# Hybrid diffusion trunk on one core: the context queries of the even layer's attention issued inside the last HGRN unit, the output weights split during the latent queries

## The chip, the cores and the metric

The kernel runs on one NeuronCore of a Trainium2 chip. A core has five engines that each work through a queue of their own in order: TensorE (PE, matrix products into PSUM), VectorE (DVE), ScalarE (ACT), GpSimd (POOL) and SyncE (SP, which here only issues DMA transfers). They meet through semaphores. The metric is the device time of one execution in microseconds; lower is better. All matrix work is done in float32 by splitting an operand into a high part `hi` (rounded by a cast on ACT) and a low part `lo` (the difference, by a subtraction on DVE or POOL), and adding three products.

## The reference, cut to what matters

Two layers over 1024 latent tokens and 256 context tokens of width 1024. The change lies in the mixer of layer 0 (the even layer), where two mixers work side by side and one output projection joins them:

```
def attend(q, k, v):                          # mixer A: 8 query heads, 2 key heads, head size 64
    s = einsum("bqhgd,bkhd->bhgqk", q, k) * ATTN_SCALE
    p = softmax(s)
    return einsum("bhgqk,bkhd->bqhgd", p, v)
o_lat = attend(q_lat, concat(k_ctx, k_lat), concat(v_ctx, v_lat))   # latent queries: all 1280 keys
o_ctx = attend(q_ctx, k_ctx, v_ctx)                                 # context queries: 256 keys

def step(S, inp):                             # mixer B (HGRN2): 4 heads, both directions
    scores = einsum("bhtd,bhtsd,bhsd->bhts", qc, decay, kc)
    o = einsum("bhts,bhsv->bhtv", scores, vc) + einsum("bhtd,bhdv->bhtv", qc * exp(b), S)
    S_new = exp(b_last) * S + einsum("bhsd,bhsv->bhdv", kc * exp(b_last - b), vc)

y = concat([o_attention, rms_norm(o_hgrn) * silu(g)]) @ w_out       # for latent and context tokens
```

Then come a gated FFN, the odd layer and its FFN; none of them is touched.

## The kernel before

**Stages.** `even_in` holds the first 630 us: the token-major projections (`even_token_major`, which writes queries, keys and values to the DRAM scratch `q2d`, `k2d`, `v2d`) and the HGRN mixer (`hgrn`). `even_out` holds the attention and the output projection (`even_attention`), to about 1085 us. `second` is everything after.

**HGRN.** There are 12 units: 4 heads times three token blocks (context 256, latent 512, latent 512). For each unit, `project(u)` makes the products with the operands `xh`, `xl` (5 KB of each partition per 1280 tokens and eight slices, 80 KB in all) and the split weights; `chain(u)` runs the log-step scan within chunks of 128 tokens: seven levels (m = 1, 2, 4, ... 64), each with one product group on PE (tiles `h_pd`, `h_pa`), one copy `hKM` on ACT for m up to 16, and three products on DVE (`hK` L795, `hQ` L797, `hT` L798); then transposes `h_kt`, the masked sum `hA` (L824 to L836). `tail(u)` makes the chunk states (`h_ds`, `hds`, `hS` L928), the outputs `h_po`, the RMS norm over `h_ms`, `h_dg`, `h_bc` and the gating on POOL (L977), and stores to `hgd`. `chain(u)`, `tail(u - 1)` and `project(u + 1)` are issued in turns: a `yield` of one is followed by steps of the others. The last unit has no `project` beside it, so its chain and its tail are alone on the engines.

**Attention.** `even_attention` works through 40 pairs of (block of 256 queries, head): 8 context pairs first, then 32 latent ones. The loop runs over half-steps `s`; half-step `s` issues the scores of tile `s` (two tiles of 128 queries make a pair), the exponential of tile `s-1` (L1054, ACT), the transposes of pair `s//2 - 2` (`a_pt`), their split into `a_ph` (ACT) and `a_pl` (DVE L1082), the products with the values of pair `s//2 - 3` (`a_pv`), the division of tile `s-1` by its sum (reciprocal `rl` L1059 on DVE, scaling L1060 on POOL) and, at the end of a pair, `finish` (`pv_t` on ACT, `a_oT` on DVE L1111). The row maximum is taken by one DVE instruction that also moves the scores to SBUF (`a_p<-g_ps` or `a_p<-a_s`, L1047). Half-steps 0 to 15 are the context pairs (256 keys); half-step 16 is the first with latent queries (1280 keys). Two steps of the output projection (three products each) go into each half-step once a block's eight heads and its four HGRN slices (`a_g`, loaded from `hgd`) are split.

**Output weights.** `even_w_out` is split in 8 pieces: `load_w(m)` loads a 512 KB `w_raw`, `prepare_w(m)` casts `w_hi` on ACT (L1018) and subtracts `w_lo` on POOL (L1019), then issues `load_w(m + 2)`. Piece m is prepared in half-step 2m + 2, all within the context pairs. `w_raw` and `a_g` share a tag with two buffers.

**Order.** Inside `in_order(...)` every instruction of the engines named keeps the order in which the code issues it; between two such blocks a scheduler may move an instruction. `chained()` keeps the order of SP's transfers. A tile that takes over the memory of an earlier one waits until the last reader of that one is done. When `even_in` closes, `even_out` opens its pools over the same SBUF and PSUM.

Of the kernel before, what the change touches and what calls it, by code (L numbers as in the profile page):

```python
# [20 lines left out]
P = 128  # L21
# [44 lines left out]
class Trunk:  # L66
# [597 lines left out]
    def hgrn(self, xh, xl, gp):  # L664
# [73 lines left out]
        first, tp, pp, sp, mods = yield load, prepare, project  # L738
# [8 lines left out]
        def chain(u):  # L747
# [11 lines left out]
            pd = [pp.tile([P, 2, 5, 32], F32, name=f"h_pd{i}", bufs=1) for i in range((nch + 1) // 2)]  # L759
# [126 lines left out]
        with self.in_order(*self.compute):  # L886
# [6 lines left out]
            for u in range(len(units)):  # L893
                fill = project(u + 1) if u + 1 < len(units) else iter(())
# [13 lines left out]
                for _ in fill:  # L908
                    x += 1
                    if x % 2 == 0:  # L910
                        side()
            while tails:
                side()
            for _ in mods:
                pass
# [66 lines left out]
    def even_attention(self, gp, tp, pp, sp):  # L982
# [32 lines left out]
        def prepare_w(m):  # L1015
# [3 lines left out]
            nc.gpsimd.tensor_tensor(out=lo, in0=raw, in1=hi.bitcast(F32), op=OP.subtract)  # L1019
# [5 lines left out]
        def load_keys(g):  # L1025
            for s in range(2):
                k = K2[g, s] = sp.tile([P, NTOK], F32R, name=f"K2_{g}{s}", bufs=1)
                nc.sync.dma_start(k.bitcast(F32), self.k2d[g, s].bitcast(F32))
# [39 lines left out]
        def transposes(pair, half):  # L1068
# [66 lines left out]
        def project():  # L1135

            for b, (n0, kind) in enumerate(blocks):
                for i in range(2):
                    y = sp.tile([P, D], F32, name="y", bufs=2)
                    ms = self.small.tile([P, 2], F32, name="y_ms")  # L1140
                    for half in range(2):
# [11 lines left out]
                        if half == 0:  # L1153
                            xt = sp.tile([P, D], F32, name="y_x", bufs=2)
# [33 lines left out]
        nc.gpsimd.memset(zeros, 0.0)  # L1188
        N = 2 * len(pairs)
        E = mybir.EngineType  # L1190
        with self.in_order(*self.compute, E.SP):
            load_keys(0)
            load_q(0)
            load_q(1)
            load_keys(1)
            V = sp.tile([P, NT, AKV * P], F32R, name="V2", bufs=1)
            nc.sync.dma_start(V.bitcast(F32), self.v2d.rearrange("t p c -> p t c").bitcast(F32))
            load_w(0)
            load_w(1)
            load_gate(1)  # L1200
            for s in range(N + 8):
                pair, half = s // 2, s % 2
                if s < N:
                    if half == 0:
                        load_q(pair + 2)
                    scores(s)
                if 0 <= s - 1 < N:
                    exponential(s - 1)
                if 2 <= s < 18 and half == 0:
                    prepare_w(s // 2 - 1)  # L1210
                if 0 <= pair - 3 < len(pairs):
                    values(pair - 3, half)
                t = transposes(pair - 2, half) if 0 <= pair - 2 < len(pairs) else iter(())
                next(t, None)
                step(1)
                next(t, None)
                step(1)
                next(t, None)
                if 0 <= s - 1 < N:
                    divide(s - 1)  # L1220
                if 0 <= pair - 3 < len(pairs) and half == 1:
                    finish(pair - 3)
                for _ in range(min(len(todo), 1 + len(todo) // 3)):
                    todo.pop(0)()
# [1354 lines left out]
    def run(self, stages=5):  # L2579
        for f in (self.even_in, self.even_out, self.second)[:stages]:  # L2580
            f()
# [9 lines left out]
    def even_in(self):  # L2591
        nc, a, pool = self.nc, self.a, self.pool
        with ExitStack() as es:
            self.mc = pool(es, "modc")
            hp = pool(es, "h0")
            xh = hp.tile([P, KT, NTOK], F32R, name="xh")
            xl = hp.tile([P, KT, NTOK], F32R, name="xl")
            self.wp = pool(es, "weights", side="right")
            gp = pool(es, "g_psum", 2, space=PSUM)
# [159 lines left out]
```

## Time and profile before

| | |
|---|---|
| runs shown | 3350.71, 3346.67, 3350.41 us; median 3350.41 |
| the profiled execution | 3351.56 us; span of its trace 3349.8 us |
| TensorE | busy 3107.8 us (93% of the span), mean granted clock 0.967 |
| VectorE, ScalarE, GpSimd | busy 60%, 45%, 46% of the span |
| the chain that ended last | PE 73%, DVE 9%, ACT 4%, issue 3%, DMA 2% |
| PE busy, 600 to 700 us | 68.31 us, granted clock 0.76 |
| PE busy, 500 to 600 and 700 to 800 us | 89.55 us and 87.67 us |

"Busy" is the time in which an engine executes; the rest is waiting. The profile's views that are used: the windows (busy time per stretch), the timeline (single instructions with their start and duration in us, and in square brackets how long the engine was idle before and what ended that), the chain of waits, and the groups by source line (smallest, median and largest duration in ns). All three runs and the profiled execution lie within 5 us.

### The profile page before, as it was taken

The page shows a single profiled execution, that of the slowest core. Times are in us where ns is not written, and L with a number is a line of the kernel's source. Part 1 is how long each engine was busy: PE and PEld are TensorE (multiplying, and loading weights), DVE is VectorE, ACT ScalarE, POOL GpSimd, SP SyncE. Part 2 cuts the span into 40 slices and gives each one's busy share as a digit, 9 for nine tenths or more (in the row PEclk, how much of TensorE's full clock was granted, in tenths as well). Part 3 has the DMA queues.
Part 4 walks back from the last instruction along what each step waited for, and adds up shares of the span by engine and source line. Part 5 has one row for each costly group of instructions (what it writes and reads, how often), then busy time and mean ns, then how long its engine had stood idle before and what let it go on. Part 6 is the DMA issues. An engine that isn't in the chain of part 4 may idle for free.

```text
span 3349.8 us, 48795 instructions
## 1 busy us (share of the span) xinstructions
PE 3107.8 (93%) x18364; PEld 2556.4 (76%) x18364; DVE 2021.9 (60%) x3405; ACT 1502.5 (45%) x2681; POOL 1546.9 (46%) x1173
## 2 busy tenths in 40 slices
PE   7989998779998799999999989999998989999997
PEld 4766776568887588888878768889986768888785
DVE  4356566557775755454477763477775465555777
ACT  3222222266665534343344442466665534434443
POOL 1120111187774466666510111577775367777101
PEclk8999999889999899999999989999998989999998
DMA  6533343221123221121285772222224222222855
GB/s 246 195 100 127 123 127 110 85 96 45 58 68 126 72 74 70 62 74 70 88 288 189 257 238 108 80 64 62 61 72 163 84 69 79 89 79 88 286 180 206
DMA packets 202540, 398.73 MB, mean 119 GB/s; under 512 B 23344, under 2 KB 84784, under 8 KB 202304
## 3 DMA queue, kind: packets, MB, share of 16 engines
q1 hardware_dynamic: 191680, 358.38, 32.1%
q0 software_dynamic: 10624, 37.23, 2.9%
q8 instruction: 144, 2.36, 0.3%
q14 instruction: 92, 0.75, 0.1%
HBM read 316.86 MB, written 79.06 MB: 118 GB/s over the span
## 4 chain that ended last, share of the span: by engine, by line
PE 73%; DVE 9%; ACT 4%; issue 3%; DMA 2%; POOL 1%; SPq 0%; POOLq 0%; ACTq 0%; DVEq 0%
PE g_ps L136 18%; PE u_g L136 14%; PE d_ps L136 11%; PE u_v L136 10%; PE u_pc L136 4%; PE a_pv L136 2%; PE c_pv L136 2%; PE c_s L136 2%; PE c_pt L2394 2%; PE a_pt L1080 2%; DVE a_pl L1082 1%; PE o_ps L136 1%; PE a_s L136 1%; PE mod_ps L136 1%; ACT a_ph L1081 1%
## 5 line engine op out<-in xcount | busy, mean ns | idle before, releaser
L144 POOL TENSOR_TENSOR rs_r<-rs_e,mhalf 128x1 f32<-128x1 f32 (+3 forms) x106 | 81.8, 772 | 938.5 <-DVE rs_e L143 884.6
L136 PE MATMUL d_ps<-d_Bh,d_Ah 128*128 128x512 f32 x704 | 277.9, 395 | 11.3 <-ACT d_Bh L1809 11.2
L136 PE MATMUL d_ps<-d_Bl,d_Ah 128*128 128x512 f32 x704 | 278.4, 395 | 3.8 <-DVE d_Bl L1810 3.8
L136 PE MATMUL d_ps<-d_Bh,d_Al 128*128 128x512 f32 x704 | 277.2, 394 | 2.0 <-DVE d_Al L1810 1.9
L2377 POOL TENSOR_SCALAR c_p<-c_p,rl 128x640 f32<-128x640 f32 (+1 forms) x128 | 232.5, 1818 | 95.6 <-DVE rl L2376 63.6
L1060 POOL TENSOR_SCALAR a_p<-a_p,rl 128x1280 f32<-128x1280 f32 (+1 forms) x80 | 240.2, 3008 | 55.5 <-DVE rl L1059 48.4
L136 PE MATMUL g_ps<-xh,w_hi 128*128 128x512 f32 (+1 forms) x640 | 259.6, 406 | 3.6 <-DVE hq L711 2.2
L136 PE MATMUL g_ps<-xh,w_lo 128*128 128x512 f32 (+1 forms) x640 | 239.7, 375 | 0.8 <-POOL w_lo L2277 0.8
L136 PE MATMUL g_ps<-xl,w_hi 128*128 128x512 f32 (+1 forms) x640 | 240.2, 375 | 0.0
L1082 DVE TENSOR_TENSOR a_pl<-a_pt,a_ph 128x512 fp32r<-128x512 f32 (+1 forms) x200 | 118.9, 602 | 92.1 <-ACT a_ph L1081 92.0
L1497 DVE TENSOR_TENSOR f_u<-u_v,f_p 128x512 f32<-128x512 f32 x88 | 60.5, 687 | 184.3 <-PE u_v L136 184.3
L136 PEld LDWEIGHTS d_ps<-d_Bh,d_Ah 128*128 128x128 f32 x704 | 133.8, 190 | 41.9 <-ACT d_Bh L1809 12.8
L1483 POOL TENSOR_TENSOR w_S4l<-w_s,w_S4h 128x512 fp32r<-128x512 f32 x44 | 57.2, 1299 | 229.5 <-ACT w_S4h L1482 229.5
L136 PEld LDWEIGHTS d_ps<-d_Bl,d_Ah 128*128 128x128 f32 x704 | 134.0, 190 | 36.1 <-DVE d_Bl L1810 7.6
L136 PEld LDWEIGHTS d_ps<-d_Bh,d_Al 128*128 128x128 f32 x704 | 133.9, 190 | 30.9 <-DVE d_Al L1810 3.3
L136 PEld LDWEIGHTS g_ps<-xh,w_hi 128*128 128x128 f32 x640 | 123.6, 193 | 42.6 <-issue 27.7
L1081 ACT CAST a_ph<-a_pt 128x512 fp32r<-128x512 f32 (+1 forms) x200 | 101.9, 518 | 108.3 <-PE a_pt L1080 108.2
L2397 DVE TENSOR_TENSOR c_pl<-c_pt,c_ph 128x256 fp32r<-128x256 f32 (+1 forms) x256 | 112.9, 469 | 58.3 <-ACT c_ph L2396 57.1
L136 PE MATMUL g_ps<-w_hi,xh 128*128 128x512 f32 (+1 forms) x368 | 143.5, 390 | 4.8 <-DVE xh L2151 2.1
L136 PEld LDWEIGHTS g_ps<-xh,w_lo 128*128 128x128 f32 x640 | 123.0, 192 | 24.0 <-POOL w_lo L2277 1.2
L136 PE MATMUL g_ps<-w_lo,xh 128*128 128x512 f32 (+1 forms) x368 | 137.5, 374 | 4.0 <-DVE w_lo L2138 2.9
L2396 ACT CAST c_ph<-c_pt 128x256 fp32r<-128x256 f32 (+1 forms) x256 | 98.4, 414 | 90.8 <-PE c_pt L2394 88.7
(543 smaller groups left out, 9884.6 us busy)
## 6 DMA issues: line engine op xcount, KB each, us to landing
m_raw<-in_w_mod SPq DMA_DIRECT2D x96, 512.0 KB
w_raw<-in_w_up SPq DMA_DIRECT2D x88, 512.0 KB
d_rawA<-actd SPq DMA_DIRECT2D x77, 512.0 KB
d_rawB<-in_w_down SPq DMA_DIRECT2D x74, 512.0 KB
actd<-f_t SPq DMA_DIRECT2D x22, 640.0 KB
d_t<-in_w_down SPq DMA_DIRECT2D x22, 512.0 KB
actd<-f_t SPq DMA_DIRECT2D x22, 512.0 KB
d_s<-actd SPq DMA_DIRECT2D x20, 512.0 KB
```

Source lines behind the costliest of these rows:

```text
L136: return self.nc.tensor.matmul(out, lhsT, rhs, start=start, stop=stop, skip_group_check=True, **k)
L144: nc.gpsimd.tensor_tensor(out=r[:p, :n], in0=e[:p, :n], in1=self.mhalf[:p, :n], op=OP.pow)
L1060: nc.gpsimd.tensor_scalar(Pt[:, :nk], Pt[:, :nk], rl, None, op0=OP.mult)
L1080: nc.tensor.transpose(pt[:, m, qt * P:(qt + 1) * P], Pt[:, kts[j + m] * P:(kts[j + m] + 1) * P], self.ident)
L1081: nc.scalar.copy(ph[:, j:j + n], pt[:, :n])
L1082: nc.vector.tensor_tensor(out=pl[:, j:j + n], in0=pt[:, :n], in1=ph[:, j:j + n].bitcast(F32), op=OP.subtract)
L1483: nc.gpsimd.tensor_tensor(out=lo, in0=part(j, name), in1=hi.bitcast(F32), op=OP.subtract)
L1497: nc.vector.tensor_tensor(out=out, in0=x, in1=y, op=OP.add)
L2377: nc.gpsimd.tensor_scalar(Pt[:, :n], Pt[:, :n], rl, None, op0=OP.mult)
L2394: nc.tensor.transpose(pt[:, j, :], Pt[:, (src + j) * P:(src + j + 1) * P], self.ident)
L2396: nc.scalar.copy(vap(ph, o, dims), pt[:, :cnt])
L2397: nc.vector.tensor_tensor(out=vap(pl, o, dims), in0=pt[:, :cnt], in1=vap(ph, o, dims).bitcast(F32), op=OP.subtract)
```

## The change

The two stages become one function, `even`. `even_attention` becomes a generator that the HGRN loop drives:

- When the last unit's projection has been issued, the memory of `xh`, `xl` and of the projection weights is given up (`left.close()`), and the attention's tiles are laid over it. The HGRN's own tiles move to the other side of SBUF, the projection weights and `xh`, `xl` to the left.
- The last unit's chain runs outside the loop: after each of its ten steps except the ninth, `more()` issues one half-step of the attention; during the tail each step is followed by one more, up to half-step 15. Half-steps 16 and later stand where they stood, after the tail.
- Keys and values are loaded in two portions: the context columns first, the latent columns after them.
- Context pairs put their product with the values in the two-buffer tile `g_ps` and not in `a_pv`, and finish half a pair earlier. In the tail the transposes use the banks of `h_pa`, `h_pd0`, `h_pd1` in turn.
- The split of the output weights moves from half-steps 2 to 16 to half-steps 16 to 23, one piece in each, and the even pieces' `w_lo` is subtracted on DVE. A projection step waits in the issue order until its piece is there.
- `zeros` is set on DVE, and `y_x` gets a pool of its own.

Names and line numbers of the instructions shift by some twenty lines; up to the last unit's chain each engine's order is otherwise the same.

**VectorE at the start of the last chain.** Before (`hkd`, `hQ`, `hK`, `hT` are the chain's tiles):

```order
L754 TENSOR_TENSOR hkd<-hK 128x512
L756 TENSOR_TENSOR hQ<-hq,hF 128x512
L757 TENSOR_TENSOR hQ<-hq,hF 128x512
L795 TENSOR_TENSOR hK<-hK,hF 128x2x256
L797 TENSOR_TENSOR hQ<-hQ,hF 128x2x256
L798 TENSOR_TENSOR hT<-hF 128x2x256
L795 TENSOR_TENSOR hK<-hK,hT 128x2x128x2
```

With the change:

```order
L754 TENSOR_TENSOR hkd<-hK 128x512
L756 TENSOR_TENSOR hQ<-hq,hF 128x512
L757 TENSOR_TENSOR hQ<-hq,hF 128x512
L1069 ISA a_p,nm<-g_ps,zeros 128x256
L1069 ISA nm 128x1
L796 TENSOR_TENSOR hK<-hK,hF 128x2x256
L798 TENSOR_TENSOR hQ<-hQ,hF 128x2x256
L799 TENSOR_TENSOR hT<-hF 128x2x256
L1069 ISA a_p,nm<-g_ps,zeros 128x256
L1069 ISA nm 128x1
L1081 RECIPROCAL rl<-l 128x1
L796 TENSOR_TENSOR hK<-hK,hT 128x2x128x2
```

Each level of the chain now has a row maximum (`a_p,nm`) and a reciprocal `rl` ahead of it in the queue; the first of them waits for scores, and the scores for the first keys.

**SyncE around the output weights.** Before (`a_q` are query tiles, `gate` the modulation gate):

```order
L1028 DMA K_11_6573<-k2d 128x1280
L1197 DMA V_6575<-v2d 128x10x256
L1013 DMA w_raw<-in_even_w_out 128x2x512 x2
L1003 DMA gate<-gated 128x1024
L998 DMA a_q<-q2d 128x256 x2
```

With the change (from the third query pair on; `a_g` is the context block's HGRN output):

```order
L1024 DMA gate<-gated 128x1024
L1019 DMA a_q<-q2d 128x256 x8
L1034 DMA w_raw<-in_even_w_out 128x2x512 x2
L1019 DMA a_q<-q2d 128x256
L1034 DMA w_raw<-in_even_w_out 128x2x512
L1143 DMA a_g<-hgd 128x256 x4
L1034 DMA w_raw<-in_even_w_out 128x2x512
L1019 DMA a_q<-q2d 128x256
L1034 DMA w_raw<-in_even_w_out 128x2x512 x2
```

`a_g` now comes between the pieces. It takes the second of the two buffers after piece 1 and keeps it until half-step 22, so that in the built program pieces 2 to 7 all lie in the first one (byte 155520 of a partition; `a_g` at 159616). The load of each of them waits for the `w_lo` of the piece before: on DVE for pieces 3, 5 and 7, on POOL for 4 and 6.

**ScalarE in half-steps 18 to 21, with the change** (`w_hi` is the cast of a piece, `a_ph` the high part of the transposes, `a_p,l` the exponential):

```order
L1039 CAST w_hi<-w_raw 128x1024
L1107 CAST a_ph_6970<-a_pt 128x512
L1135 COPY pv_t<-g_ps 64x256
L1076 ACTIVATE a_p,l<-a_p,nm 128x1280
L1039 CAST w_hi<-w_raw 128x1024
L1076 ACTIVATE a_p,l<-a_p,nm 128x1280
L1039 CAST w_hi<-w_raw 128x1024
L1107 CAST a_ph_7032<-a_pt 128x512 x2
L1107 CAST a_ph_7032<-a_pt 128x256
L1135 COPY pv_t<-g_ps 64x256
```

The casts stand ahead of the half-step's `a_ph`; before, they stood between the much shorter context half-steps.

The core of the diff (`hgrn`, then `even_attention`, then `even`):

```diff
-            for u in range(len(units)):
-                fill = project(u + 1) if u + 1 < len(units) else iter(())
+            for u in range(len(units) - 1):
+                fill = project(u + 1)
...
+            att, done = attention(), []
+            def more():
+                if not done and next(att) == "end":
+                    done.append(1)
+            more()
+            x = 0
+            for _ in chain(len(units) - 1):
+                side()
+                if x != 8:
+                    more()
+                side()
+                x += 1
+            self.a_pt = pp
             while tails:
                 side()
-            for _ in mods:
-                pass
+                more()
...
-            nc.gpsimd.tensor_tensor(out=lo, in0=raw, in1=hi.bitcast(F32), op=OP.subtract)
+            (nc.gpsimd if m % 2 else nc.vector).tensor_tensor(out=lo, in0=raw, in1=hi.bitcast(F32), op=OP.subtract)
...
-                pt = tp.tile([P, 2, QB], F32, name="a_pt", tag="tp")
+                if self.a_pt:
+                    self.a_tag = (self.a_tag + 1) % 3
+                    pt = self.a_pt.tile([P, 2, QB], F32, name="a_pt", tag=("h_pa", "h_pd0", "h_pd1")[self.a_tag], bufs=1)
+                else:
+                    pt = tp.tile([P, 2, QB], F32, name="a_pt", tag="tp")
...
-                st["pv"] = pp.tile([P, 512], F32, name="a_pv", bufs=1)
+                st["pv"] = gp.tile([P, 512], F32, name="g_ps") if blocks[b][1] else pp.tile([P, 512], F32, name="a_pv", bufs=1)
...
-                if at[0] < 32 * (st.get("ready", -1) + 1):
+                if at[0] < 32 * (st.get("ready", -1) + 1) and (at[0] >= 16 or at[0] // 2 < len(W)):
...
+        def half_step(s):
...
+            if 16 <= s < 24:
+                prepare_w(s - 16)
...
+            if 0 <= p3 < len(pairs) and half == 1 - blocks[pairs[p3][0]][1]:
+                finish(p3)
...
+            load_keys(0, ctx)
             load_q(0)
             load_q(1)
-            load_keys(1)
+            load_keys(1, ctx)
             V = sp.tile([P, NT, AKV * P], F32R, name="V2", bufs=1)
-            nc.sync.dma_start(V.bitcast(F32), self.v2d.rearrange("t p c -> p t c").bitcast(F32))
+            for t in (slice(8, 10), slice(0, 8)):
+                nc.sync.dma_start(V[:, t].bitcast(F32), self.v2d[t].rearrange("t p c -> p t c").bitcast(F32))
+                if t.start:
+                    load_keys(0, lat)
+            load_keys(1, lat)
+            load_gate(1)
+        yield
+        for s in range(16):
+            with self.chained():
+                half_step(s)
+            yield
+        pp, yp = yield "end"
+        with self.in_order(*self.compute, E.SP):
             load_w(0)
             load_w(1)
-            load_gate(1)
-            for s in range(N + 8):
...
-                if 2 <= s < 18 and half == 0:
-                    prepare_w(s // 2 - 1)
...
+            for s in range(16, N + 8):
+                half_step(s)
...
+            def attention():
+                left.close()
+                return self.even_attention(gp, tp, pool(es, "at", 2))
...
+            top.close()
+            right.close()
             self.weights(es, 2, 8)
+            yp = pool(es, "y_x", side="right")
             pp = pool(es, "at_psum", 1, space=PSUM)
```

More of the change, by code (lines that the diff above doesn't have):

```diff
@@ L735, in project @@
             nc.sync.dma_start(V[:, :n // P, :], self.bid.rearrange("t p c -> p t c")[:, n0 // P:(n0 + n) // P, h * P:(h + 1) * P])
-        first, tp, pp, sp, mods = yield load, prepare, project
+        first, tp, pp, sp, mods, attention = yield load, prepare, project
         M1 = sp.tile([P, P], F32, name="hM1", bufs=1)
@@ L911, in hgrn @@
                         side()
+            for _ in mods:
+                pass
+            att, done = attention(), []
[11 more added lines that the diff above has]
+            self.a_pt = pp
             while tails:
                 side()
-            for _ in mods:
-                pass
+                more()
+            while not done:
+                more()
+            self.a_pt = None
+        return att
     def hgrn_states(self, st, S, d, sp):
@@ L1198, in even_attention @@
+        yield
+        for s in range(16):
+            with self.chained():
+                half_step(s)
+            yield
+        pp, yp = yield "end"
+        with self.in_order(*self.compute, E.SP):
             load_w(0)
             load_w(1)
-            load_gate(1)
-            for s in range(N + 8):
[L1202 to L1208, printed above, removed]
-                if 2 <= s < 18 and half == 0:
-                    prepare_w(s // 2 - 1)
[L1211 to L1224, printed above, removed]
@@ L2579, in run @@
     def run(self, stages=5):
-        for f in (self.even_in, self.even_out, self.second)[:stages]:
+        for f in (self.even, self.second)[:stages]:
             f()
```

89 lines of the change are left out of this document (55 added, 34 removed).

## The prediction

> **What bounds the kernel now.** I read the windows first, to see whether the place has time to give. Columns: stretch, its length, busy us of PE, its weight loads, DVE, ACT and POOL with their instructions, PE's granted clock, DMA share, GB/s.
>
> ```profile
> 500.00:600.00 100.00, 89.55 (x974) 67.39 (x973) 60.37 (x130) 27.17 (x52) 12.62 (x16) 0.97 0.34 111
> 600.00:700.00 100.00, 68.31 (x710) 53.94 (x708) 54.49 (x140) 36.77 (x77) 41.29 (x43) 0.76 0.35 118
> 700.00:800.00 100.00, 87.67 (x544) 75.25 (x543) 71.88 (x135) 65.00 (x123) 81.37 (x35) 0.97 0.14 44
> ...
> 630.00:640.00 10.00, 3.50 (x178) 2.77 (x178) 8.87 (x17) 2.53 (x4) 0.00 (x0) 0.70 1.00 374
> 640.00:650.00 10.00, 6.71 (x58) 5.79 (x58) 7.49 (x17) 2.34 (x4) 0.00 (x0) 0.62 0.02 6
> ```
>
> PE bounds the neighbours, but not 600 to 700: 68.31 us busy at a clock of 0.76. In 630 to 640 it is DVE (8.87 of 10). Next the timeline, for landmarks. DVE, last unit: start of the chain, first level, masked sum, last product of the tail.
>
> ```profile
> 628.77 0.69 DVE L754 TENSOR_TENSOR hkd<-hK 128x512 f32<-128x512 f32 x1
> 630.59 0.68 DVE L795 TENSOR_TENSOR hK<-hK,hF 128x512 f32<-128x512 f32 x1
> ...
> 645.25 0.68 DVE L824 TENSOR_TENSOR hA<-h_pa,hM 128x512 f32<-128x512 f32 x1
> ...
> 667.45 0.75 DVE L976 SCALAR_TENSOR_TENSOR h_part<-h_bc,onw,h_part 128x512 f32<-128x512 f32 x1 [3.91 <-PE h_bc L136]
> ```
>
> PE: scores of a context pair, of half-step 16 (the first latent one), and of 24 with the transposes that follow.
>
> ```profile
> 686.02 1.20 PE L136 MATMUL g_ps<-K,a_q 128*128 128x256 f32 x4
> ...
> 698.76 2.29 PE L136 MATMUL a_s<-K,a_q 128*128 128x512 f32 x6
> ...
> 732.02 1.41 PE L136 MATMUL a_s<-K,a_q 128*128 128x512 f32 x6
> ...
> 735.00 0.60 PE L1080 MATMUL a_pt<-ident,a_p 128*128 128x128 f32 x4
> ```
>
> So there are three stretches: the last chain, 628.8 to 645.25 (16.5 us); its tail, to 668.2 (23 us); and from there to the scores of half-step 24, 63.8 us with all eight context pairs and the first eight latent half-steps. From 732 on PE runs at its bound (87.67 busy in 700 to 800, with the slow start in it), so I take half-step 24 as the mark: a shift there reaches the end. The chain of waits tells what the third stretch consists of:
>
> ```profile
> 668.23 4.13 DMA w_raw<-in_even_w_out
> 672.38 1.05 ACT w_hi L1018
> 673.51 2.35 POOL w_lo L1019
> ...
> 688.84 1.20 PE a_pv L136 x4
> 690.03 0.87 PE a_pt L1080 x4
> 690.98 0.59 ACT a_ph L1081
> ...
> 697.21 3.88 DMA w_raw<-in_even_w_out
> ```
>
> **Term 1: the chain, +11.** DVE's queue gets eight half-steps, in a stretch where it has little room. One costs these rows: a row maximum and its read-out, a reciprocal; per pair also a_pl and a_oT.
>
> ```profile
> 687.08 0.69 DVE L1082 TENSOR_TENSOR a_pl<-a_pt,a_ph 128x512 fp32r<-128x512 f32 x1 [2.44 <-ACT a_ph L1081]
> 687.68 0.15 DVE L1059 RECIPROCAL rl<-l 128x1 f32<-128x1 f32 x1
> 687.75 0.41 DVE L1047 CUSTOM_DVE_ANT_0 a_p<-g_ps,zeros 128x256 f32<-128x256 f32 x1
> 688.08 0.08 DVE L1047 DVE_READ_ACCUMULATOR2_ANT nm<- 128x1 f32 x1
> ...
> 688.27 0.42 DVE L1111 TENSOR_TENSOR a_oT<-a_pv,pv_t 64x256 f32<-64x256 f32 x1
> ```
>
> Eight times (0.41 + 0.08 + 0.15 rounded up to 0.66) is 5.3; two a_pl and one a_oT 1.8. Waits come on top, since the order puts them ahead of the chain's own products. The keys are first loaded when the last projection has read `xh`:
>
> ```profile
> 627.35 0.82 SPq L1028 DMA_DIRECT2D K<-k2d  x2
> 628.22 1.08 SPq L998 DMA_DIRECT2D a_q<-q2d  x2
> ```
>
> and DMA first moves data at 628. I let the first queries land 2.2 us after their issue, at 630.5: the first scores end near 631.8, the row maximum near 632.4, and hK follows there and not at 630.59: 1.8. Its bounds are 0 and 4.1 (the w_raw row). The table of the exponential, loaded in an idle stretch before, now stands between an hKM copy and the reciprocal that DVE waits for:
>
> ```profile
> 658.88 1.28 ACT L1054 ACT_TABLE_LOAD   x1
> ```
>
> 1.2 of it shows. The third pair's queries stand on SP behind all keys, values and the gate. Sizes of one issue:
>
> ```profile
> K<-k2d SPq DMA_DIRECT2D x4, 640.0 KB
> a_q<-q2d SPq DMA_DIRECT2D x14, 128.0 KB
> V<-v2d SPq DMA_DIRECT2D x1, 1280.0 KB
> gate<-gated SPq DMA_DIRECT2D x1, 512.0 KB
> ```
>
> Before, four K, V and two a_q, 4.2 MB, kept the DMA engines busy to 640 (share 1.00 and 374 GB/s, then 0.02); the gate and one a_q, 0.65 MB, add 1.8 at that rate, which ends near 642 to 643, just after DVE gets to half-step 4: 0.9 (bounds 0 and 4). Sum 1.8 + 1.2 + 5.3 + 1.8 + 0.9 = 11.0: hA at 656.3.
>
> **Term 2: the tail, +15.** Half-steps 8 to 15 are four pairs. The tail is a string of round trips PE, ACT, DVE; each pair puts another in front in the same queues: scores 0.6 (half the 1.20 of a pair), values 1.20, transposes 0.87, a_ph 0.59, a_pl 0.69, reciprocal 0.15, a_oT 0.42: 4.5 us. Four make 18. The bounds are 0 (all inside the tail's idle time, such as DVE's 3.91 above) and 18; I take 15, since most of these wait on each other in queue order: hS waits for an hds copy that stands behind a_ph, pv_t and a_oh on ACT, and the next scores behind h_po. The tail ends at 668.2 + 26 = 694.2. The scores of half-step 16 stand a little before that, near 689 instead of 698.76; term 3 takes this lead back.
>
> **Term 3: from the tail's end to half-step 24, 47.7 instead of 63.8.** The context pairs are gone from here, but eight pieces of output weights have come, and pieces 2 to 7 pass through one buffer. Each piece is: load, cast on ACT, subtract, and only then the next load. The casts stand ahead of each half-step's a_ph, so ACT, and with it the transposes, waits for every load. DVE's price for a subtraction of this size, and POOL's for what stands around its own:
>
> ```profile
> L685 DVE TENSOR_TENSOR w_lo<-w_raw,w_hi x16: 1224/1225/2367, 157.8 to 521.4; 128x1024 fp32r<-128x1024 f32 x16
> L1060 POOL TENSOR_SCALAR a_p<-a_p,rl x80: 914/3522/3562, 671.9 to 1037.5; 128x1280 f32<-128x1280 f32 x64, 128x256 f32<-128x256 f32 x16
> L1101 POOL TENSOR_TENSOR a_ol<-a_oT,a_oh x20: 727/737/767, 690.0 to 1056.0; 128x256 fp32r<-128x256 f32 x20
> ```
>
> Piece 0's w_lo follows the tail's last product: 1.2. Six loads at 4.0 (rows 4.13 and 3.88): 24. Six casts at 1.05: 6.3. Pieces 2, 4, 6 on DVE: 3.7; pieces 3, 5 on POOL at 2.35: 4.7. Waits inside the loop: the cast of piece 2 behind the exponential of half-step 17, 2.3; piece 5 on POOL behind one a_p (3.52), partly over: 3.7 with an a_ol. Hand-overs 1.0, and after the last cast an a_ph and a transpose, 0.8. Sum 47.7: half-step 24 at 741.9, against 732.02.
>
> **Costed at nothing.** `zeros` on DVE, one column, no more than the 0.08 of the read-out row; the finer pools and the other sides of SBUF, which leave the order before the last chain alone; the projection of the context block, which begins one half-step earlier but is paced by the half-steps. POOL's context work (16 times 0.91 for the scaling) hides: POOL had 0.00 in 630 to 650. If it did not, a 0.91 for each of the eight in the chain is 7.3, and that is in the third rival.
>
> **The sum.** 11.0 + 15 + 47.7 - 63.8 = +9.9 us. The profiled execution took 3351.56, so 3361.5; its time lies 1.15 above the median of the runs shown (3350.41), so against that median it is 3360.3. I say 3361. The likeliest case's own range is 3354 to 3370: term 2 by 4 either way, the load by 0.5 six times.
>
> **Rivals.**
>
> *A, faster: the idle time swallows the half-steps.* Place: the tail. For it: DVE has 3.58 busy of 10 in 650 to 660 and 1.67 in 660 to 670, PE ran at a clock of 0.50 for much of it and would run its part quicker when fuller. Against it: each queue is in order, and the pairs depend on three engines in turn. Then term 2 is 0 and of term 1 only DVE's own 5.3 is left: 5.3 + 47.7 - 63.8 = -10.8, so 3340.8. It decides from the point where the stretch of chain and tail falls below 16.1 us (63.8 - 47.7).
>
> ```profile
> 650.00:660.00 10.00, 5.64 (x42) 5.26 (x42) 3.58 (x11) 2.97 (x4) 3.20 (x5) 0.89 0.00 0
> 660.00:670.00 10.00, 5.62 (x12) 2.72 (x12) 1.67 (x3) 0.16 (x1) 6.87 (x10) 0.50 0.13 32
> ```
>
> *B, about the same: the loads do not pace, POOL does.* If loads come well ahead of their casts, half-step 24 waits for POOL's scaling of tiles 20 and 21. From the tail's end POOL does the last gating and its store (1.25 below, and about 1), one short a_p at 0.91, five a_ol at 0.74, three w_lo at 2.35 and six a_p at 3.52: 35. The transposes of half-step 24 begin 3 us after its scores (732.02 and 735.0), so those stand at 694.2 + 32 = 726.2: -5.8, 3346. Against it: the loads' waits are in the built program.
>
> ```profile
> 668.30 1.25 POOL L977 TENSOR_TENSOR h_part<-h_part,hgate 128x512 f32<-128x512 f32 x1 [0.91 <-DVE h_part L976]
> ```
>
> *C, slower still: DVE and POOL block each other.* Two rows show one instruction with two lengths:
>
> ```profile
> L327 DVE SCALAR_TENSOR_TENSOR y<-y,rs_r,gate x10: 1276/1777/1789, 787.9 to 1083.0; 128x1024 f32<-128x1024 f32 x10
> L385 POOL TENSOR_TENSOR qk<-qk_n,rCq x8: 1289/1788/1796, 161.3 to 215.6; 128x512 f32<-128x512 f32 x8
> ```
>
> Each is 0.5 us longer than its shortest, and L327 runs beside POOL's a_ol, L385 beside a DVE product. The chain's products (two inputs in SBUF) now run beside eight scalings, four w_lo on DVE beside a_p of 3.52. Eight times 0.55 and four times half an a_p (1.76): 4.4 + 7.0 = +11.4 on the forecast, 3373. The L685 row has a case of 2367 for it; against it, most of its cases are at 1225. The Trainium skill, "SBUF — State Buffer", section "Who interferes with whom", says that a DVE instruction with two SBUF inputs and a GpSimd instruction that reads SBUF exclude each other, the later one waiting for the whole of the other; by that rule the sum would be this rival's, and the 0.5 of the two rows agrees in kind.
>
> **Chances.** What a measurement here can tell from no change is about 0.2%, 6.7 us: faster is below 3343.7, slower above 3357.1. Forecast 0.48 (0.40 slower, 0.08 within); A 0.22 (0.17 faster, 0.05 within); B 0.12 (0.05 faster, 0.07 within); C 0.18, slower. Together faster 0.22, same 0.20, slower 0.58. The range 3339 to 3377 reaches through A and past C; outside lie a term 1 of 0 as well (below) and a lock on every product (above).
>
> **What would show it.** Term 1: hA some 27 us after hkd, not 16.5. Term 2: the last h_part product near 694. Term 3: w_raw loads 2 to 7 issued one by one, 6 to 10 us apart, ACT waiting for DMA at each w_hi, half-step 24 near 742. A would show as h_part before 684, B as w_hi that never waits for DMA, C as hK, hQ or w_lo rows far above 0.69 and 1.23. The forecast is wrong if half-step 24 stands before 732, or if time is lost or won elsewhere than between 628 and 742.

## The result and the profile after

| | before | with the change |
|---|---|---|
| median of 7 runs | 3347.48 us (3342.58 to 3350.71) | 3358.24 us (3355.42 to 3359.97) |
| profiled execution, its span | 3351.56, 3349.8 us | 3356.05, 3354.3 us |
| busy TensorE, mean granted clock | 3107.8 us, 0.967 | 3106.9 us, 0.966 |

The ratio is 1.0031, with a 95% interval of 1.0019 to 1.0043: slower by 0.31%. The forecast was +9.9 us (0.30%). The two profiled executions differ by 4.5 us only; executions of one kernel lie 8 us apart in these runs and up to 16 in the later ones, so the amount is taken from the medians and the place from the traces.

The windows of the kernel with the change, columns as before:

```profile
600.00:700.00 100.00, 72.43 (x742) 58.78 (x741) 63.15 (x158) 38.65 (x83) 37.78 (x40) 0.81 0.27 94
700.00:800.00 100.00, 80.12 (x452) 69.53 (x451) 61.80 (x111) 56.62 (x103) 74.07 (x30) 0.83 0.20 64
```

PE is fuller by 4.1 us in the first stretch (68.31 before) and emptier by 7.6 us in the second (87.67 before). The gap has moved from the chain and tail into the latent half-steps. The landmarks: on VectorE the start of the chain, the row maximum of half-step 4 with its wait, the masked sum, the tail's last product:

```profile
628.00 0.69 DVE L754 TENSOR_TENSOR hkd<-hK 128x512 f32<-128x512 f32 x1
...
644.58 0.42 DVE L1069 CUSTOM_DVE_ANT_0 a_p<-g_ps,zeros 128x256 f32<-128x256 f32 x1 [5.23 <-PE g_ps L136]
...
655.05 0.67 DVE L825 TENSOR_TENSOR hA<-h_pa,hM 128x512 f32<-128x512 f32 x1
...
690.89 0.75 DVE L997 SCALAR_TENSOR_TENSOR h_part<-h_bc,onw,h_part 128x512 f32<-128x512 f32 x1 [3.23 <-PE h_bc L136]
```

On PE the scores of half-steps 16 and 24:

```profile
684.62 1.39 PE L136 MATMUL a_s<-K,a_q 128*128 128x512 f32 x6
...
739.11 1.40 PE L136 MATMUL a_s<-K,a_q 128*128 128x512 f32 x6
```

And what the chain of waits shows between them:

```profile
633.63 10.07 DMA a_q<-q2d
...
709.95 3.75 DMA w_raw<-in_even_w_out
713.72 1.05 ACT w_hi L1039
714.80 1.24 DVE w_lo L1040
716.05 3.89 DMA w_raw<-in_even_w_out
...
723.39 2.35 POOL w_lo L1040
725.76 3.79 DMA w_raw<-in_even_w_out
729.57 1.05 ACT w_hi L1039
```

Load, cast, subtraction, next load: the string that term 3 forecast. The table sets beside these two kernels those of the experiments below. All stretches are measured from hkd, since hkd itself lies between 624.6 and 630.3 in these executions. Columns: hkd to hA; hA to the tail's end; hkd to the scores of half-step 16; from there to those of 24; hkd to 24; from the row maximum of 24 to that of 32; hkd to the row maximum of 40; ratio to the kernel before, with its interval.

| kernel | chain | tail | to 16 | 16 to 24 | to 24 | 24 to 32 | to 40 | ratio |
|---|---|---|---|---|---|---|---|---|
| before | 16.48 | 22.95 | 69.99 | 33.26 | 103.25 | 40.8 | 189.28 | 1 |
| the change | 27.05 | 36.59 | 56.62 | 54.49 | 111.11 | 41.1 | 199.51 | 1.0031 [1.0019, 1.0043] |
| e_q | 22.71 | 36.87 | 52.56 | 55.11 | 107.67 | 41.1 | 195.97 | 1.0017 [1.0008, 1.0027] |
| e_g | 27.68 | 35.73 | 57.10 | 49.25 | 106.35 | 41.1 | 194.80 | 1.0024 [1.0012, 1.0036] |
| e_notail | 26.39 | 27.18 | 66.47 | 50.79 | 117.26 | 41.1 | 205.64 | 1.0041 [1.0028, 1.0055] |
| e_nochain | 17.74 | 28.60 | 59.29 | 53.22 | 112.51 | 41.1 | 199.29 | 1.0028 [1.0018, 1.0038] |
| e_bw | 15.94 | 22.95 | 70.32 | 48.67 | 118.99 | 40.8 | 205.05 | 1.0037 [1.0024, 1.0051] |
| e_pool | 26.54 | 36.72 | 56.23 | 58.19 | 114.42 | 41.3 | 202.30 | 1.0035 [1.0023, 1.0046] |
| e_qgd | 22.44 | 37.81 | 53.70 | 49.68 | 103.38 | 41.1 | 191.79 | 1.0018 [1.0008, 1.0027] |
| e_spread | 27.10 | 36.46 | 56.51 | 43.79 | 100.30 | 42.8 | 188.78 | 0.9993 [0.9983, 1.0002] |
| e_qspread | 22.64 | 38.23 | 54.32 | 43.25 | 97.57 | 42.9 | 186.14 | 0.9982 [0.9973, 0.9991] |
| e_qsp_pool | 22.58 | 36.81 | 52.37 | 44.25 | 96.62 | 41.2 | 185.06 | 0.9976 [0.9966, 0.9985] |
| e_qspl | 23.08 | 36.72 | 52.78 | 41.98 | 94.76 | 53.9 | 195.61 | 1.0014 [1.0005, 1.0023] |
| e_even_pool | 21.95 | 37.78 | 53.20 | 41.16 | 94.36 | 48.8 | 188.89 | 0.9987 [0.9977, 0.9997] |

The second row against the first is nearly the whole case: half-step 16 comes 13.4 us earlier, and the eight half-steps behind it take 21.2 us longer, which leaves +7.9 at half-step 24. By half-step 40 it is +10.2. From there to the row maximum of half-step 79 each of these executions takes 209.1 to 209.4 us, so what a kernel wins or loses in the attention is settled at 40.

Two cautions. The five kernels that differ only in what they do from half-step 16 on (e_q, e_qspread, e_qsp_pool, e_qspl, e_even_pool) reach half-step 16 between 52.4 and 54.3 us after hkd, so a landmark that moves by less than 2 us shows nothing by itself. And each ratio is taken against runs of the kernel before from the same session, whose medians lie between 3347.1 and 3349.4.

### The profile page after: what moved, and what is told of

Read it like the earlier page. It is cut to its first block, busy times and chain, and to the rows that moved or that the text cites. A ratio compares the mean times of both kernels' runs of the same rounds, so it can differ in the third digit from the quotient of the medians.

```text
span 3354.3 us, 48782 instructions
## 1 busy us (share of the span) xinstructions
PE 3106.9 (93%) x18364; PEld 2559.1 (76%) x18364; DVE 2025.4 (60%) x3410; ACT 1501.5 (45%) x2681; POOL 1543.0 (46%) x1168
## 4 chain that ended last, share of the span: by engine, by line
PE 72%; DVE 9%; ACT 4%; issue 3%; DMA 3%; POOL 1%; SPq 1%; POOLq 0%; ACTq 0%; DVEq 0%
PE g_ps L136 18%; PE u_g L136 14%; PE d_ps L136 11%; PE u_v L136 11%; PE u_pc L136 4%; PE a_pv L136 2%; PE c_pv L136 2%; PE c_s L136 2%; PE c_pt L2438 2%; PE a_pt L1106 2%; DVE a_pl L1108 1%; PE o_ps L136 1%; PE mod_ps L136 1%; PE a_s L136 1%; ACT a_ph L1107 1%
## 5 line engine op out<-in xcount | busy, mean ns | idle before, releaser
L136 PEld LDWEIGHTS d_ps<-d_Bh,d_Ah 128*128 128x128 f32 x704 | 133.3, 189 | 40.4 <-ACT d_Bh L1853 11.4
```

The lines of the kernel that those rows point to most:

```text
L136: return self.nc.tensor.matmul(out, lhsT, rhs, start=start, stop=stop, skip_group_check=True, **k)
```

## The experiments

**Loads on their own: e_q and e_g.** In e_q the third query pair is asked for among the first keys, not behind 4.7 MB:

```diff
             load_keys(1, ctx)
+            load_q(2)
```

> The third query pair's load is issued among the first keys, ahead of the latent keys, values and the gate. Theory (in-order transfers): the 5.2 us that VectorE waits ahead of the row maximum of half-step 4 go; the fourth pair's queries still come behind the 4.7 MB, but half-step 6 then stands near 643 and waits at most 1 us. hA 22 to 23 us after hkd instead of 27.05, half-step 24 some 4 us earlier, time 3358 - 4 = 3354. Rival (the wait was cover for something else in the chain, or the same wait only goes to half-step 6): hA still 26 to 27 us after hkd, time 3358.

Measured: 3354.21 us; hA at 22.71; half-step 24 3.4 us earlier. VectorE no longer waits at half-step 4, and at half-step 6 it waits 0.78. As the theory had it.

In e_g the context block's `a_g` leaves the buffers of `w_raw`:

```diff
-                g = st["g", b] = self.wp.tile([P, BH, QB], F32, name="a_g", tag="w_raw", bufs=2)
+                g = st["g", b] = (self.wp if b else sp).tile([P, BH, QB], F32, name="a_g", tag="w_raw" if b else "y", bufs=2)
```

> a_g of the context block takes a buffer of y instead of one of w_raw, so that the eight pieces of output weights alternate between two buffers. Theory (single-buffered loads pace the third stretch): ScalarE's waits of 4.38, 5.44 and 3.33 us ahead of w_hi go, GpSimd's idle 9.6 us in 696 to 738 is used; tail's end to half-step 24 falls from 47.5 to 38 to 40 us; time 3358 - 8 = 3350. Rival (GpSimd or the order of the casts paces it, loads are hidden anyway): not below 45 us, time 3356 or more.

Measured: 3354.24 us; tail's end to half-step 24 42.9, between the two. ScalarE's waits for a piece fell from 13.7 us to 4.5 (2.93 and 1.56), but only 4.5 of the 8 us expected came; the rest is taken over by GpSimd and by VectorE's subtraction. Of e_g, the timeline: GpSimd's scaling, VectorE's subtraction beside it, and PE, which waits for the `a_pl` queued behind:

```profile
725.05 3.52 POOL L1082 TENSOR_SCALAR a_p<-a_p,rl 128x1280 f32<-128x1280 f32 x1
...
725.53 3.68 DVE L1040 TENSOR_TENSOR w_lo<-w_raw,w_hi 128x1024 fp32r<-128x1024 f32 x1
...
729.86 0.44 PE L1106 MATMUL a_pt<-ident,a_p 128*128 128x128 f32 x2 [3.70 <-DVE a_pl L1108]
```

**The place of the context pairs: e_notail and e_nochain.** One leaves the half-steps out of the tail, the other out of the chain; what is left out follows behind the tail.

```diff
             while tails:
                 side()
-                more()
```

> No half-step is issued during the tail; half-steps 9 to 15 follow it. Theory (each pair costs a round trip wherever the engines' queues are in order): the tail is back near 23 us after hA (-13.6), the seven half-steps behind it cost 1.2 to 1.9 us each (8 to 13), half-step 24 0 to 5 us earlier than with the change, time 3353 to 3358: the tail swallows nothing. Rival (the tail's idle time does hide part of them): half-step 24 later by 4 us or more, time 3362.

Measured: 3362.06 us; half-step 24 6.2 us later: the rival. Without them the tail is 27.2 (the theory had 23; the `a_pl` and `a_oT` of one pair still fall into it), so the seven cost 9.4 inside it (36.59 less 27.18); behind it they take 12.9, and half-step 16 no longer begins 7.0 before the tail's end. With the seven inside the tail half-step 16 comes 9.9 us earlier, and 3.7 of that is lost again by half-step 24 (54.49 against 50.79).

```diff
-                if x != 8:
-                    more()
```

> No half-step is issued during the chain; eight or so go into the tail, the others follow it. Theory: hA is back at 16.5 us after hkd (-10.6), the tail costs 36 us as with the change, the eight half-steps behind it cost 1.2 to 1.9 us each (10 to 15): half-step 24 within -1 to +5 us of the change, time 3357 to 3363. Rival (the chain hides nothing, its half-steps cost more there than anywhere): half-step 24 earlier by 4 us or more, time 3354.

Measured: 3355.66 us, half-step 24 1.4 us later, as the theory had the landmark, but its parts and its time (3357 to 3363) missed: the tail took 28.6 and not 36, and half-step 16 begins 13.0 behind its end. The time, 2.6 below the change's median, is inside the scatter. Whether the chain is the right place for eight of them makes no difference that shows here.

**The weights' new place alone: e_bw.** The kernel before, with only its pieces moved:

```diff
-                if 2 <= s < 18 and half == 0:
-                    prepare_w(s // 2 - 1)
+                if 16 <= s < 24:
+                    prepare_w(s - 16)
```

and even pieces on VectorE, and the rule that holds back a projection step, as in the change.

> The kernel before with one part of the change alone: the output weights are split in half-steps 16 to 23, one piece in each, even pieces on VectorE; the context pairs stay behind the tail. Theory (the weights' new place is what costs): the sixteen context half-steps, relieved of w_lo, take 20 to 24 us from the tail's end instead of 30.6; half-steps 16 to 24 take 50 to 54 us instead of 33.3; half-step 24 stands 113 to 117 us after hkd (before 103.25, the change 111.1), time 3347 + 11 = 3358. Rival (the long latent half-steps come from the pairs' earlier place): half-steps 16 to 24 stay below 40 us, time 3340 to 3347.

Measured: 3361.42 us; 16 to 24 takes 48.67 instead of 33.26, half-step 24 at 118.99. So this part alone puts half-step 24 later than the whole change does. But the context half-steps took 31.4 us and not 20 to 24: a miss, and with it the landmark (113 to 117 expected). GpSimd in that stretch, of the kernel before and then of e_bw (its busy time stands ahead of the clock):

```profile
670.00:700.00 30.00, 17.28 (x76) 14.53 (x76) 12.54 (x53) 20.45 (x50) 27.95 (x24) 0.61 0.59 192
```

```profile
670.00:700.00 30.00, 18.96 (x75) 16.67 (x76) 12.38 (x54) 13.96 (x43) 13.22 (x15) 0.51 0.26 88
```

GpSimd falls from 93% busy to 44% and the stretch gets no shorter. The chain of waits of e_bw says why:

```profile
683.01 1.19 PE a_pv L136 x4
684.20 0.87 PE a_pt L1080 x4
685.14 0.59 ACT a_ph L1081
...
686.52 0.16 DVE a_p L1047
686.96 0.43 DVE a_oT L1111
687.52 1.20 PE a_pv L136 x4
...
692.04 1.20 PE a_pv L136 x4
```

One pair is a round trip PE, ACT, DVE of 4.5 us (683.01, 687.52, 692.04). The kernel before has the same period, with the weights inside, by its PE timeline:

```profile
681.50 1.20 PE L136 MATMUL g_ps<-K,a_q 128*128 128x256 f32 x4
...
686.02 1.20 PE L136 MATMUL g_ps<-K,a_q 128*128 128x256 f32 x4
...
690.54 1.20 PE L136 MATMUL g_ps<-K,a_q 128*128 128x256 f32 x4
```

Before the change the split of the weights cost nothing: it filled the idle time of a round trip. The change moved it to where it is waited for.

**Who subtracts: e_pool and e_qgd.** e_pool puts all eight `w_lo` back on GpSimd; e_qgd takes e_q and e_g and puts all on VectorE.

```diff
-            (nc.gpsimd if m % 2 else nc.vector).tensor_tensor(out=lo, ...)
+            nc.gpsimd.tensor_tensor(out=lo, ...)
```

> The change with all eight w_lo on GpSimd, as before the change. Theory (VectorE's subtractions are cheap here because GpSimd mostly idles beside them: three rows of 1.21 to 1.23 us and one of 1.63): four times 1.15 us more on GpSimd, and a load that waits for GpSimd's queue instead of VectorE's, behind an a_p of 3.5: half-steps 16 to 24 rise from 54.5 to 59 to 66 us, time 3358 + 8 = 3366. Rival (VectorE and GpSimd shut each other out, so that half of the pieces on VectorE brings nothing): 54 us or less, time 3358 or less.

> The change with the third pair's queries loaded among the first keys, a_g of the context block in a buffer of y, and all eight w_lo on VectorE. Theory (with two buffers GpSimd's queue paces the third stretch): without its 2.4 to 3.2 us pieces half-steps 16 to 24 fall from the 49.3 of the two-buffer run to 43 us, half-step 24 stands 96 to 99 us after hkd, time 3345. Rival (VectorE and GpSimd exclude each other, the w_lo only move the wait): w_lo rows of 3 us and more, as one of 3.59 in the two-buffer run, half-steps 16 to 24 not below 48 us, time 3350.

Measured: e_pool 3361.1 us, 16 to 24 58.2: the half on VectorE gains 3.7 us there, less than the theory's 4.5 to 11.5. e_qgd 3354.77 us, 16 to 24 49.7, no better than e_g's 49.25: the rival. Its `w_lo` rows on VectorE have a mean of 1973 ns (eight of them, up to 3.00 us). Taking 2.4 us pieces from GpSimd gains nothing while VectorE stands still beside its scalings. e_qgd reaches half-step 24 where the kernel before does and still ends 0.18% later: 2.1 us of that come in half-steps 32 to 40, which took it 45.6 us against 43.6 (as they took the change; the reason stands under the sum below). The rest of the 5.5 us between the medians is open.

**Spread pieces: e_spread and e_qspread.** One piece in every second half-step, and in e_qspread the early third queries as well. Piece m is first needed at half-step 24 + m, by its projection product:

```diff
-            if 16 <= s < 24:
-                prepare_w(s - 16)
+            if s in (16, 17, 19, 21, 23, 25, 27, 29):
+                prepare_w((s - 15) // 2)
```

> The change with the pieces of output weights split in half-steps 16, 17, 19, 21, 23, 25, 27 and 29 instead of 16 to 23; single buffer as it is. Theory (one piece in every half-step is what the load, cast and subtraction round trip can't keep up with): no wait of ScalarE for w_raw over 1 us, half-steps 16 to 24 fall from 54.5 to 37 to 41 us, and from 24 on nothing is lost; time 3358 - 15 = 3343. Rival (the pieces cost the same wherever they are split, GpSimd having no room in half-steps 24 to 30 either): half-step 32 no more than 5 us earlier than with the change, time 3354.

> The same, and the third pair's queries loaded among the first keys. Theory: the two gains add, 3358 - 15 - 3.5 = 3339 to 3340, faster than the kernel before. Rival (what is won before half-step 24 is lost behind it): 3347 to 3350.

Measured: 3348.13 and 3343.2 us (3343 and 3339 to 3340 expected). ScalarE waits for no piece any more; 16 to 24 is 43.8 us, 10.7 shorter but not the 37 to 41 expected, and 24 to 32 1.6 longer. The theory holds with two thirds of its size; e_qspread is faster than the kernel before by 0.18%.

**The last steps: e_qsp_pool, e_qspl, e_even_pool**, all on top of e_qspread. The first has all `w_lo` on GpSimd, with the edit of e_pool.

> The spread pieces with the early third queries, and all eight w_lo on GpSimd. Theory (in the spread kernel three of four w_lo on VectorE take 2.16 to 2.56 us beside a scaling of 3.5 and hold back a_pl and with it the transposes): those three waits go and half-steps 24 to 28 fall from 22.2 to 20.5 us, as before the change; but GpSimd has 4 x 2.38 more in half-steps 16 to 24, where it is already the engine waited for: half-step 24 2 us later; time 3343. Rival (GpSimd sets the pace up to half-step 30): half-step 32 4 us later or more, 3347.

Measured: 3341.07 us, ratio 0.9976; 24 to 32 back at 41.2, half-step 24 0.95 earlier rather than 2 later. That last is no gain of the edit: half-step 16, ahead of it, stood 1.95 earlier, and 16 to 24 took 1.0 longer. It beats the kernel before and the change; against e_qspread (0.9982) the intervals overlap. GpSimd now has all the long work, and VectorE no subtraction that GpSimd could hold up.

e_qspl moves `prepare_w` of e_qspread behind the half-step's transposes and scaling:

```diff
-            if s in (16, 17, 19, 21, 23, 25, 27, 29):
-                prepare_w((s - 15) // 2)
             p3, p2 = pair - 3, pair - 2
...
                 divide(s - 1)
+            if s in (16, 17, 19, 21, 23, 25, 27, 29):
+                prepare_w((s - 15) // 2)
```

> The spread pieces with the early third queries; cast and subtraction of a piece stand behind the half-step's transposes, a_ph, a_pl and scaling instead of ahead of them. Theory (the cast ahead of a_ph and the subtraction ahead of a_pl cost their own length, 1.0 and 1.2 to 2.5 us, in each half-step with a piece): half-steps 16 to 24 2 to 4 us shorter, 24 to 28 1 us shorter, time 3340. Rival (GpSimd's scalings set the pace, the order on the other engines is hidden): within 1 us of the spread run, 3343.

Measured: 3353.49 us; half-step 24 is 2.8 us earlier, 1.3 of it between 16 and 24 (2 to 4 expected), but 24 to 32 takes 53.9. Neither theory had that. The timeline of e_qspl:

```profile
747.95 3.52 POOL L1082 TENSOR_SCALAR a_p<-a_p,rl 128x1280 f32<-128x1280 f32 x1 [0.95 <-DVE rl L1081]
748.21 3.88 DVE L1040 TENSOR_TENSOR w_lo<-w_raw,w_hi 128x1024 fp32r<-128x1024 f32 x1 [0.45 <-ACT w_hi L1039]
752.13 0.42 DVE L1137 TENSOR_TENSOR a_oT<-a_pv,pv_t 64x256 f32<-64x256 f32 x1
...
752.60 0.58 PE L136 MATMUL a_pv<-a_ph,V 128*128 128x256 f32 x1 [4.61 <-DVE a_oT L1137]
```

The subtraction now begins right behind the start of a scaling and in front of `a_oT`; `a_pv` has one buffer, so PE stands for 4.61 us, in the stretch where PE is the bound. Behind it PE stands for another 2.63 us, for the last piece. The waits are not all: from the row maximum of 24 to that of 32 the same 256 products are busy 3.9 us longer, at a lower granted clock. e_qspread, then e_qspl (PE's is the first pair, the clock the third number from the end):

```profile
724.80:767.65 42.85, 39.97 (x256) 34.66 (x256) 32.12 (x57) 29.79 (x54) 34.78 (x14) 1.00 0.23 79
```

```profile
727.00:780.87 53.87, 43.88 (x256) 38.04 (x256) 33.59 (x58) 29.04 (x54) 34.40 (x14) 0.90 0.19 64
```

e_even_pool is e_qsp_pool with the pieces in half-steps 16, 18, to 30, four instead of five ahead of 24:

```diff
-            if s in (16, 17, 19, 21, 23, 25, 27, 29):
-                prepare_w((s - 15) // 2)
+            if 16 <= s < 32 and half == 0:
+                prepare_w(s // 2 - 8)
```

> As the spread kernel with all w_lo on GpSimd, but the pieces in half-steps 16, 18, 20, up to 30: four of them ahead of half-step 24 instead of five. Theory (GpSimd, which never idles over 0.2 us between 690 and 729 in that run, sets the pace there): one w_lo of 2.35 less, half-step 24 2 to 2.4 us earlier, nothing lost behind it, time 3341 - 2 = 3339. Rival (the round trip of load and cast, with its wait of 0.62, or VectorE and ScalarE set the pace): half-step 24 within 0.7 us, time 3341; the last piece, at half-step 30 for products of half-step 31, comes late: 3343 or more.

Measured: 3346.04 us (3339 expected). Half-step 24 is 2.3 us earlier, as the theory said of GpSimd, which in e_qsp_pool has 18.72 and then 20.00 of 20 us:

```profile
680.00:700.00 20.00, 12.90 (x49) 9.57 (x48) 11.34 (x25) 11.29 (x19) 18.72 (x17) 0.80 0.26 86
700.00:720.00 20.00, 12.41 (x58) 10.64 (x56) 9.18 (x17) 10.08 (x20) 20.00 (x8) 0.74 0.21 66
```

But 24 to 32 takes 48.8: the last piece comes late, as the rival's second half had it. Of the 7.7 us more than in e_qsp_pool, 2.7 are the same products at a lower clock. Of e_even_pool, GpSimd and PE:

```profile
758.43 3.52 POOL L1082 TENSOR_SCALAR a_p<-a_p,rl 128x1280 f32<-128x1280 f32 x1 [0.67 <-DVE rl L1081]
...
762.60 2.34 POOL L1040 TENSOR_TENSOR w_lo<-w_raw,w_hi 128x1024 fp32r<-128x1024 f32 x1
...
764.99 0.80 PE L136 MATMUL g_ps<-w_lo,a_oh 128*128 128x512 f32 x1 [3.02 <-POOL w_lo L1040]
```

## Why the prediction was right, step by step

**Term 1, +11: measured +10.6** (27.05 less 16.48), but with other parts. The first keys cost 0 and not 1.8: the first row maximum stands right behind `hQ`. The table of the exponential cost 1.11 (1.2 forecast). VectorE's added busy time was 5.2, not 7.1, and its idle time grew by 5.4. The windows of the chain, of the kernel before and then with the change (VectorE's is the third pair):

```profile
628.77:645.25 16.48, 6.58 (x247) 5.23 (x247) 13.01 (x25) 3.11 (x5) 0.00 (x0) 0.66 0.68 252
```

```profile
628.00:655.05 27.05, 14.13 (x278) 11.25 (x277) 18.18 (x51) 9.81 (x24) 9.88 (x6) 0.60 0.55 190
```

Two waits for `a_ph` of 1.0 and 1.2 were not in the list, and 3.5 us of idle time stood in the chain before. The third pair's queries were the mis-sized part: 0.9 forecast with a bound of 4, 5.23 measured. They landed at 643.70, close to where the working had them (642 to 643), but VectorE stood at half-step 4 near 639 already, since it had lost less ahead of it. A landing fixes the time; what was too much ahead of it only shortened the wait. That is why the sum held though most of its parts were off, and e_q shows it: without this landing the chain is 4.3 us shorter.

**Term 2, +15: measured +13.6** (36.59 less 22.95), inside its 4 either way. Its reason, that a pair costs its round trip of 4.5 in the tail, was too simple: e_notail shows that the tail hides a good part of the pairs, if what they would cost elsewhere is counted, and in e_nochain ten row maxima, three `a_pl` and two `a_oT` lengthen the tail by 5.7 only. The working took that as the lead of half-step 16 (near 689 forecast, 684.62 measured).

**Term 3, 47.7: measured 47.5**, with half of the mechanism as forecast: single loads of 3.75 to 3.89 us (4.0 taken), issued 6.1 to 9.7 us apart, with ScalarE waiting 4.38, 5.44 and 3.33 us at pieces 3, 4 and 6. Pieces 2 and 5 had no wait, and piece 7 one of 0.52, so the sign "at each w_hi" held for four of six. The agreement of the size is in good part luck. The chain of waits between 691.64 and 739.11 holds three loads with 11.4 us, where the term had six with 24; GpSimd holds 12.1 us of it (8.4 forecast), PE 5.9 (next to nothing forecast), and 8.3 are "issue", time for which the profile shows no wait. e_g bears this out by half: a second buffer gives 4.5 us, not 8. The granted clock in this stretch was 0.68 (0.76 in the old one), which can have lengthened only PE's 5.9 of the chain.

**The sum.** Half-step 24 was to be 9.9 later; it was 7.9 from hkd, and medians differ by 10.8. A reading beside the sum failed: that the weights' split belonged to the price of the old third stretch. e_bw shows that it was free there.

The rest comes behind the mark. The prediction let a shift at half-step 24 reach the end unchanged, put the earlier start of the context block's projection at nothing, and named time lost outside 628 to 742 as a sign of being wrong. Half-steps 32 to 40, from 782 to 828, took 45.6 us instead of 43.6. There PE waits for `a_oT`, which stands on VectorE behind two products of the projection's output. Timeline of the change:

```profile
789.96 1.28 DVE L327 SCALAR_TENSOR_TENSOR y<-y,rs_r,gate 128x1024 f32<-128x1024 f32 x1
...
791.76 1.22 DVE L1188 TENSOR_TENSOR y<-y,y_x 128x1024 f32<-128x1024 f32 x1
...
793.88 0.47 PE L136 MATMUL a_pv<-a_ph,V 128*128 128x256 f32 x1 [2.04 <-DVE a_oT L1137]
```

In the kernel before these two come one half-step later, and PE's waits for `a_oT` there are 0.28 each. e_nochain has the same wait of 2.04 and takes 44.0 us, 0.5 more than the kernel before; the other 1.6 us are the half-step behind the wait, which ran at a lower clock in the change (last section). e_bw, with only the weights moved, keeps the waits of 0.28 and the 43.6. That the projection's place causes the wait is read from the traces; no run moved it alone. So the sum, +9.9 against +10.8, is closer than its parts: 2.0 too much at its own mark, and 2.3 behind it that it had put at nothing.

**Rival A** (the idle time swallows the half-steps) asked that chain and tail take less than 16.1 us more; they took 24.2, and it fell. **Rival B** (GpSimd paces) fell in part for the change: ScalarE did wait for DMA, but GpSimd holds as much of the chain as the loads. It is what bounds once the loads are out of the way: e_qsp_pool and e_even_pool show GpSimd full up to half-step 24. **Rival C** (GpSimd and VectorE block each other) fell by place: the chain's `hK` rows stayed at 0.67 to 0.70, and of the four `w_lo` on VectorE three took 1.21 to 1.23, two of these with GpSimd idle beside them, since everything waited for the load. Where a `w_lo` on VectorE meets a scaling, as in e_g, e_qgd and e_qspl, it costs up to 2.7 us for a piece, and 2.8 in e_q (4.00 us).

## What to carry to other kernels

Work that fills an engine to 93% can still be free, when a round trip between other engines sets the pace around it; before it is moved, ask which period it sits in (4.5 us here, with and without it) and whether its new place has one as slack. A tile that shares a tag can turn a double buffer into a single one without a line that says so. And work which must be done by half-step 24 + m should be spread up to just ahead of that point: one piece in every half-step it cost 21 us, and moved back by up to one half-step from the best spread it cost 7.7 behind the mark. Such a mark has to be read again on its far side: here 2.3 us came behind it.

## What the runs showed of the hardware

VectorE's subtraction of two SBUF tiles (1.23 us alone) that begins inside a GpSimd scaling of 3.52 us ended 0.62 to 0.64 us behind the scaling's end, whenever it had begun, in 17 of 19 such rows between 680 and 770 us of these runs; the other two began 0.2 and 0.3 us ahead of that end. Two of them stand above: 725.53 + 3.68 against 725.05 + 3.52, and 748.21 + 3.88 against 747.95 + 3.52. The Trainium skill, "SBUF — State Buffer", section "Who interferes with whom", says that the later one waits for the whole of the other; the trace agrees that it is held to about the other's end, but only half of its own 1.23 us remains then. GpSimd's spans in the profile are rough, so the scaling may have let go earlier than its recorded end.

The other way round GpSimd gives way: five scalings of 256 columns that began inside an `hK` product of the chain (both inputs in SBUF) took 1.73 to 1.96 us, each ending 0.70 to 0.71 us behind the end of the `hQ` product that follows, while the products stayed at 0.67 to 0.69. The sixth in the chain, at 652.78, began ahead of an `hK` and took 0.92. The timeline of the kernel with the change, in the chain, and then beside products that read PSUM:

```profile
633.58 0.67 DVE L796 TENSOR_TENSOR hK<-hK,hT 128x512 f32<-128x512 f32 x1
633.83 1.73 POOL L1082 TENSOR_SCALAR a_p<-a_p,rl 128x256 f32<-128x256 f32 x1 [16.14 <-DMA K<-k2d]
...
655.30 0.92 POOL L1082 TENSOR_SCALAR a_p<-a_p,rl 128x256 f32<-128x256 f32 x1 [1.60 <-DVE rl L1081]
```

In some of these executions a wait of PE cost more than its length, as in e_qspl and e_even_pool above. In the change and in e_nochain PE waits the same 2.04 us for `a_oT`, and the half-step behind it has 34 products in both. Their rows, from one row maximum to the next, first the change and then e_nochain:

```profile
793.86:800.58 6.72, 6.70 (x34) 6.11 (x35) 3.37 (x6) 4.10 (x7) 4.54 (x4) 0.75 0.19 78
```

```profile
791.82:796.97 5.15, 5.12 (x34) 4.60 (x35) 3.38 (x6) 4.10 (x7) 4.57 (x4) 1.00 0.02 7
```

The granted clock of 0.75 makes it 1.6 us longer. Half-steps 32 to 40 took 45.5 to 45.7 us in six of the twelve kernels with the moved context pairs and 44.0 to 44.1 in the other six. Why the clock fell behind one wait and not behind the other is not shown; each kernel was profiled once.
